# Scaling a pass's tokens on one engine, and copying values in sixteen pieces: a change to the projections of an encoder block

## The chip, the cores and the metric

One core of a Trainium2 chip runs the whole kernel in one launch. The metric is the device time of an execution in microseconds (us); smaller is better.

## The reference

The block prepends 16 learned meta tokens to 2048 tokens of width 1024, normalises them, projects them once, feeds two mixers side by side (attention in a window of a grid, and a gated delta rule in both directions), projects back, and ends with a gated feed-forward layer and a last normalisation.

```python
h = jnp.concatenate([meta, x], axis=1)
u = rmsnorm(h, g_mix[l])
proj = u @ w_in[l]
na_q, na_k, na_v, dn_q, dn_k, dn_v, dn_z, dn_b, dn_a = jnp.split(proj, pts, axis=-1)
y_na = neighbourhood_attention(na_q, na_k, na_v, na_rel_bias[l], rows)
y_dn = gated_deltanet(dn_q, dn_k, dn_v, dn_z, dn_b, dn_a, ...)
h = h + jnp.concatenate([y_na, y_dn], axis=-1) @ w_out[l]
u = rmsnorm(h, g_ffn[l])
h = h + (silu(u @ w_gate[l]) * (u @ w_up[l])) @ w_down[l]
return rmsnorm(h, g_final)[:, N_META:]
```

Here `rmsnorm(x, g)` is x times the reciprocal root mean square of its row, times g. What matters below are the projection `u @ w_in` and the values `na_v` of the attention's 8 heads.

## The kernel before

The change lies in `phase_a`, the projections, which take the first 890 us or so. Work there is done in two passes, each for half of the tokens; the pass for tokens 1024 to 2047 comes first, and the second pass (from about 400 us) has tokens 0 to 1023 with the meta tokens. Tokens lie in tiles of 128; the tiles of a pass are grouped into three chunks.

**Tokens of a pass.** Both a high and a low part of each normalised token are kept in fp32r (`uh`, `ul`), and products are made three times: high by high, high by low, low by high. In the second pass the reciprocal norms are known already (`rb`, a row copied to all partitions, held in the buffer that the trace calls `gb`) and the input comes transposed, features on partitions. `put_t` (from L310) loads a tile `xt` of 128 x (8 feature blocks x 128 tokens), multiplies it by the feature gains `gc` on POOL (L321), multiplies it by `rb` on DVE (L322), casts the high part on ACT (L324), and subtracts for the low part on DVE (L325). The pool of these tiles has three buffers, so the first three tiles of the second pass are scaled long before it starts and five at its start, as the buffers come free.

**Units.** A pass is a list of units. A feature unit (`dense_feat`, products at L405) makes 128 output features for the three chunks, 72 products in all; a token unit (`run_nat`, products at L429) makes 256 or 272 output columns for each token tile, 24 products a tile. Both write an accumulator `acc` in PSUM, which has three buffers. ACT evacuates it (L447 and L472 for token units, L490 for feature units); DVE adds to some of them (L473). Behind a feature unit come a short convolution (ACT L497, DVE L499), a gate (ACT L632, DVE L633), transposes on TensorE (L639) and squares on ACT (L642). The weights of a unit are loaded ahead by `weights`: two transfers to `raw` tiles, of which there are two buffers (L236), a cast of the high part on ACT (L241, to `wf` or `wn`), and the low part on POOL (L242).

**Side work.** Between chunks, `step` (L376) advances generators that are held in `Side` queues: the weights `ws`, the work after a convolution `post`, the preparation of the delta rule `pre`, and `first`. `pre` builds triangular inverses: it loads `dx` (L840) and rows of gates (L843), stores blocks to memory and reads them back as lanes (L905 and L907 write `lane`, L916 reads the blocks `U`, `af`, `ab` from it), multiplies small blocks on TensorE (L938 and on, in three PSUM buffers `pp`) and stores `xq` (L994).

**Values.** The attention's values are projected by two token units, four heads each. `evac_v` stores each tile to `S.vn` in device memory (L456). When a unit is done, `fin_v` (L462) copies it within device memory to `S.vx`, four copies of overlapping column ranges, with 24 or 32 columns of 64 values, for four heads at a time: each is a transfer of 136 rows (4 heads x 34 grid rows) of 1536 or 2048 numbers. These are read in the attention stage, after `phase_a`.

All these transfers are issued by SyncE (SP), in its order. The order of each engine is set by a scheduler when the program is built: it simulates the program and takes ready instructions by priority, so an edit can move instructions elsewhere. Queued work then runs in that order on each engine.

Of the kernel before, what the change touches and what calls it, by code (L numbers as in the profile page):

```python
# [12 lines left out]
ALU = mybir.AluOpType  # L13
# [3 lines left out]
P = 128  # L17
# [4 lines left out]
KB = 8  # L22
# [13 lines left out]
CLO, CN = (0, 8, 24, 40), (24, 32, 32, 24)  # L36
# [10 lines left out]
def bc(ap, shape):  # L47
    return ap.to_broadcast(shape)
# [144 lines left out]
def phase_a(tc, S, x, meta, x_t, xe_t, g_mix_b, g_mix_c, w_feat, w_nat0, w_nat, conv_w, a_log, dt_bias, handover):  # L193
# [3 lines left out]
    nc = tc.nc  # L197
    with ExitStack() as es:
# [17 lines left out]
        rb, gb = gb, gb[:, 0:D]  # L216
        gc_ = sm.tile([P, KB], F32, name="gc", bufs=1)
        U = Ctx()
        post, pre, first, ws = Side(True), Side(), Side(), Side()
        behind = Behind(tc)  # L220

        def weights(u):
# [61 lines left out]
        def prep_rs():  # L284

            for jobs in half_plan(0):
                for job in jobs:
                    if job[1] == P:
                        square(job, load_x(job), 0)
                        yield  # L290
            finish_rs(0, 8, P)
            yield

        def row_rs():

            pt = ptp.tile([P, 4, P], F32, name="tp")
            nc.tensor.transpose(pt[0:17, 0], rsx[:, 0:17], S.ident)
            row = sm.tile([17, P], F32, name="rsrow", bufs=1)
            nc.vector.tensor_copy(row, pt[0:17, 0])
            h = nc.sync.dma_start(S.rs, row)  # L300
            U.xe = sm.tile([P, KB, NM + 2], F32, name="xe", bufs=1)
            yield
            flat = S.rs.rearrange("a b -> (a b)").rearrange("(o n) -> o n", o=1)
            nc.sync.dma_start(rb[:, 0:HT + 2], bc(flat[:, 0:HT + 2], [P, HT + 2]))
            nc.sync.dma_start(rb[:, HT + 2:], bc(flat[:, 16 * P:16 * P + NM], [P, NM]))
            with tc.issue_after(h.ins):
                nc.sync.dma_start(U.xe, xe_t)
                nc.sync.dma_start(gc_, g_mix_c)
            yield

        def put_t(job, ci):

            r0, np_, off, is_meta = job
            if np_ < P:
                e = U.xe[:, :, 0:NM] if is_meta else U.xe[:, :, NM:NM + 2]
                o = HT + 2 if is_meta else r0
            else:
                e = xp.tile([P, D], F32, name="xt").rearrange("p (k t) -> p k t", k=KB)
                nc.sync.dma_start(e, x_t[r0 // P])
                o = r0  # L320
            nc.gpsimd.tensor_tensor(e, e, bc(gc_.rearrange("p (k o) -> p k o", o=1), [P, KB, np_]), ALU.mult)  # L321
            nc.vector.tensor_tensor(e, e, bc(rb[:, o:o + np_].rearrange("p (o t) -> p o t", o=1), [P, KB, np_]), ALU.mult)  # L322
            uh, ul = (v[ci][:, :, off:off + np_] for v in (U.h, U.l))
            nc.scalar.copy(uh, e)  # L324
            nc.vector.tensor_tensor(ul, e, uh, ALU.subtract)  # L325

# [18 lines left out]
        def build(half, known):  # L345
            U.plan = half_plan(half)
            U.h, U.l = [], []
            for ci, jobs in enumerate(U.plan):
                U.h.append(upool.tile([P, KB, UCOL[ci]], F32R, name=f"uh{ci}"))
                U.l.append(upool.tile([P, KB, UCOL[ci]], F32R, name=f"ul{ci}"))  # L350
                if known:
                    with tc.high_priority(600):
                        for job in jobs:
                            put_t(job, ci)
                    continue
                xs = []
                for n, job in enumerate(sorted(jobs, key=lambda j: -j[1])):
                    xs.append((job, load_x(job)))
                    if ci == 0 and n == 0:
                        nc.sync.dma_start(gb, bc(g_mix_b, [P, D]))  # L360
                        load(0)
                if ci == 0:
                    nc.sync.dma_start(cw, conv_w)
                    nc.vector.tensor_scalar(cw, cw, 0.5, None, op0=ALU.mult)
                for n, (job, xt) in enumerate(xs):
                    square(job, xt, half, ci == 0 and n == 1)
                cs = [rcol(job, half) for job, xt in xs]
                if ci > 0:
                    finish_rs(min(cs), max(cs) + 1, P)
                for n, (job, xt) in enumerate(xs):  # L370
                    if ci == 0:
                        finish_rs(cs[n], cs[n] + 1, P)
                    put(job, xt, ci, half, n != 3)

        def step():
            ws.step()  # L376
            post.step()
            pre.step()
            first.step()

        def tick():
            behind.run(step)

        def drain(*sides):
            while any(s.q for s in sides):
                tick()
# [4 lines left out]
        def load(u):  # L391
            while u not in W:
                ws.step(True)
# [45 lines left out]
        def run(u, ci):  # L439
            (run_feat if units[u][0] == "f" else run_nat)(u, ci)  # L440
# [19 lines left out]
            return f  # L460

        def fin_v(h0):  # L462
            def f():
                for C in range(4):
                    nc.sync.dma_start(S.vx[C][h0:h0 + 4].rearrange("h r c d -> h r (c d)"),
                                      S.vn[h0:h0 + 4, :, CLO[C]:CLO[C] + CN[C]].rearrange("h r c d -> h r (c d)"))
            return f

        def evac_z(zi):
# [106 lines left out]
        for pi, us in enumerate(passes):  # L576
            if pi == 0:
                build(1, False)
                post.add(prep_rs())
            else:  # L580
                build(0, True)
            n = len(us)

            m = 3 if pi == 0 else 2
            groups = [list(range(m))] + [[i] for i in range(m, n)]
            for gi, grp in enumerate(groups):
                if pi == 1 and gi == len(groups) - 1:
                    drain(post, first)
                    early.close()
                    handover()  # L590
                if pi == 0 and gi == 13:
                    first.add(row_rs())
                for i in grp:
                    load(u0 + i)
                for ci in range(3):
                    for i in grp:
                        run(u0 + i, ci)
                if us.index(v0s[pi]) in grp and pi == 0:
                    pre.add(gates(tc, S, Q, 1, a_log, dt_bias))
                    pre.add(pre_unit(tc, S, Q, 0, 1), lambda: post.done >= 5)  # L600
                    pre.add(pre_unit(tc, S, Q, 1, 1), lambda: post.done >= 9)
                if us.index(v0s[pi]) in grp and pi == 1:
                    pre.add(gates(tc, S, Q, 0, a_log, dt_bias))
                    pre.add(pre_unit(tc, S, Q, 0, 0), lambda: post.done >= 17)
                    pre.add(pre_unit(tc, S, Q, 1, 0), lambda: post.done >= 21)
                    first.add(meta_state(tc, S, Q, cv, ptp), lambda: post.done >= 25)
            u0 += n
# [1264 lines left out]
@with_exitstack  # L1872
def block_kernel(ctx: ExitStack, tc: tile.TileContext, x, meta, x_t, xe_t, g_mix, g_mix_c, w_feat, w_nat0, w_nat, conv_w, rel, a_log,
                 dt_bias, norm_g, w_out, g_ffn, w_gate, w_up, w_down, g_final, out):
    S = scratch(tc, ctx)
    with ExitStack() as es:
        scratch_ab(tc, S, es)
        att = []
        phase_a(tc, S, x, meta, x_t, xe_t, g_mix, g_mix_c, w_feat, w_nat0, w_nat, conv_w, a_log, dt_bias,
                lambda: att.append(attention_loads(tc, S, es, rel)))  # L1880
        wes = ctx.enter_context(ExitStack())
        W = wes.enter_context(tc.tile_pool(name="W", bufs=2 * KEEP, side="right", reuse_waits="tile"))
        c = phase_c(tc, S, W, wes, x, w_out, g_ffn, w_gate, w_up, w_down, g_final, out)
        phase_b(tc, S, att[0], W, norm_g, lambda: next(c))
    for _ in c:
        pass
# [19 lines left out]
```

## Time and profile before

| | |
|---|---|
| median of 3 executions | 2893.03 us (2889.85 to 2894.18) |
| the profiled execution | 2883.66 us |
| its span in the trace | 2881.9 us |
| granted clock of TensorE, mean | 0.97 |
| TensorE (PE) busy | 2740.7 us, 95% |
| VectorE (DVE), ScalarE (ACT), GpSimd (POOL) busy | 61%, 41%, 26% |
| moved by DMA | 462.15 MB |

Times in the trace are counted from the start of the span. The granted clock is a share of full speed: 1.00 is 2.4 GHz, 0.50 is 1.2 GHz. A wait is idle time of an engine in front of one instruction, with what released it; "SPq" is the stream of instructions with which SyncE issues transfers. The DMA share of a stretch is the mean busy share of the core's 16 DMA engines in it.

### The profile page before, as it was taken

How to read it: one execution, taken by the hardware profiler on the slowest of the kernel's cores; microseconds unless marked ns; L12 is line 12 of the kernel's file. 1: busy time of each engine (PE TensorE's matmuls, PEld its weight loads, DVE VectorE, ACT ScalarE, POOL GpSimd, SP SyncE). 2: the span in 40 equal slices, each digit the busy share in tenths (PEclk: the TensorE clock that was granted, in tenths of full speed). 3: DMA queues.
4: the chain of work that ended last, by engine and by line, in shares of the span. 5: the costliest groups of instructions: out<-in, count | busy, mean ns of one | idle time of the engine just before them, and what ended most of it. 6: DMA issues, size and time to landing. Idle time of an engine off the chain costs nothing.

```text
span 2881.9 us, 45992 instructions
## 1 busy us (share of the span) xinstructions
PE 2740.7 (95%) x16364; PEld 2400.2 (83%) x16364; DVE 1758.0 (61%) x3916; ACT 1170.4 (41%) x2741; POOL 744.4 (26%) x809
## 2 busy tenths in 40 slices
PE   8999988988988999979999999999999999999998
PEld 8999988988888988878887888877887888888886
DVE  5897467895643556764567566554548556654354
ACT  4652333652415667752334333243434333233342
POOL 2253353341511212221134322300104322220010
PEclk9999999999989999989999999999999999999999
DMA  4675654565769888985534222246353222225452
GB/s 151 189 205 142 163 165 135 172 179 172 211 159 287 265 229 254 291 281 156 176 126 163 81 88 80 81 131 246 128 176 119 80 86 88 74 95 201 143 179 70
DMA packets 385220, 462.15 MB, mean 160 GB/s; under 512 B 93492, under 2 KB 277133, under 8 KB 383423
## 3 DMA queue, kind: packets, MB, share of 16 engines
q1 hardware_dynamic: 383262, 452.92, 51.5%
q0 software_dynamic: 1728, 6.29, 0.6%
q8 instruction: 130, 2.13, 0.3%
q14 instruction: 100, 0.81, 0.1%
HBM read 329.95 MB, written 136.95 MB: 162 GB/s over the span
## 4 chain that ended last, share of the span: by engine, by line
PE 54%; DMA 3%; DVE 2%; ACT 0%; issue 0%; POOL 0%; SPq 0%; DVEq 0%; ACTq 0%; POOLq 0%
PE pg L1609 24%; PE pg L1685 8%; PE pd L1469 6%; PE pd L1685 4%; PE tp L1685 4%; PE pd L1609 4%; DMA rt<-ut 1%; DMA z<-zx 1%; PE y L1148 1%; DMA k<-kx 0%; PE tp L1495 0%; PE tp L1416 0%; DMA qr<-qx 0%; DVE w L1453 0%; PE y L1134 0%
## 5 line engine op out<-in xcount | busy, mean ns | idle before, releaser
L405 PE MATMUL acc<-uh,wf 128*128 128x384 f32 (+5 forms) x1920 | 469.2, 328 | 2.3 <-ACT uh L342 1.1
L1609 PE MATMUL pg<-T,w 128*128 128x512 f32 x1584 | 393.2, 397 | 2.6 <-ACT T L1452 1.4
L1453 DVE TENSOR_TENSOR w<-rw,w 128x512 fp32r<-128x512 f32 x308 | 241.1, 785 | 251.4 <-ACT w L1452 250.5
L1609 PE MATMUL pg<-B,w 128*128 128x512 f32 x1584 | 388.6, 398 | 3.6 <-ACT B L1452 3.0
L1452 ACT CAST w<-rw 128x512 fp32r<-128x512 f32 x308 | 190.2, 620 | 485.5 <-PE tp L1685 253.4
L1609 PEld LDWEIGHTS pg<-B,w 128*128 128x128 f32 x1584 | 299.1, 189 | 77.9 <-ACT B L1452 3.9
L1609 PEld LDWEIGHTS pg<-T,w 128*128 128x128 f32 x1584 | 298.0, 188 | 76.4 <-ACT T L1452 1.8
L405 PEld LDWEIGHTS acc<-uh,wf 128*128 128x128 f32 x1920 | 339.5, 192 | 4.9 <-ACT uh L342 1.2
L405 PE MATMUL acc<-ul,wf 128*128 128x384 f32 (+5 forms) x960 | 312.3, 325 | 0.0
L1557 POOL TENSOR_TENSOR s<-rw 128x512 f32<-128x512 f32 x88 | 120.4, 1369 | 548.0 <-DMA rw<-in_w_gate_dram 297.8
L1685 PE MATMUL pg<-w,hT 128*128 128x512 f32 x1056 | 260.8, 395 | 1.2 <-ACT hT L1452 1.1
L1685 PEld LDWEIGHTS pg<-w,hT 128*128 128x128 f32 x1056 | 198.1, 188 | 50.0 <-ACT hT L1452 1.5
L429 PE MATMUL acc<-wn,uh 128*128 128x256 f32 (+3 forms) x1056 | 210.7, 298 | 8.5 <-DVE vs L473 8.2
L1453 DVE TENSOR_TENSOR w<-s,w 128x512 fp32r<-128x512 f32 x176 | 131.6, 750 | 137.9 <-ACT w L1452 136.8
L1452 ACT CAST w<-s 128x512 fp32r<-128x512 f32 x176 | 108.5, 620 | 233.5 <-PE pg L1609 138.4
L405 PEld LDWEIGHTS acc<-ul,wf 128*128 128x128 f32 x960 | 184.3, 192 | 1.0 <-DVE ul L343 0.2
L429 PEld LDWEIGHTS acc<-wn,uh 128*128 128x128 f32 (+1 forms) x1056 | 173.3, 197 | 11.4 <-DVE vs L473 8.7
L429 PE MATMUL acc<-wn,ul 128*128 128x256 f32 (+3 forms) x528 | 158.0, 299 | 2.3 <-DVE rx_i L58 2.3
L1469 PE MATMUL pd<-w,yh 128*128 128x512 f32 x512 | 160.0, 394 | 0.0
L499 DVE SCALAR_TENSOR_TENSOR ct<-cr,cw,ct 128x1024 f32<-128x1024 f32 (+1 forms) x96 | 136.4, 1426 | 37.7 <-ACT ct L497 36.5
L242 POOL TENSOR_TENSOR wf<-raw,wf 128x512 fp32r<-128x512 f32 x80 | 117.7, 1486 | 154.9 <-ACT wf L241 131.6
L1623 DVE TENSOR_TENSOR eg<-pg,eg 128x512 f32<-128x512 f32 x110 | 75.9, 690 | 106.4 <-PE pg L1609 106.3
(359 smaller groups left out, 5305.0 us busy)
## 6 DMA issues: line engine op xcount, KB each, us to landing
rw<-in_w_down_dram SPq DMA_DIRECT2D x88, 512.0 KB
w<-dx SPq DMA_DIRECT2D x24, 1024.0 KB
rw<-in_w_gate_dram SPq DMA_DIRECT2D x44, 512.0 KB
rw<-in_w_up_dram SPq DMA_DIRECT2D x44, 512.0 KB
hd<-eg SPq DMA_DIRECT2D x88, 256.0 KB
s<-hd SPq DMA_DIRECT2D x88, 256.0 KB
raw<-in_w_feat_dram SPq DMA_DIRECT2D x80, 256.0 KB
xq<-xq SPq DMA_DIRECT2D x32, 512.0 KB
```

The source lines that it names most:

```text
L242: nc.gpsimd.tensor_tensor(lo, raw, hi, ALU.subtract)
L405: nc.tensor.matmul(ps[:, 0:c1 - c0], hl[:, a, k, :], (U.h, U.l)[l][ci][:, k, c0:c1], start=(i == 0), stop=(i == 23))
L429: nc.tensor.matmul(ps[0:np_, 0:n], (U.h, U.l)[l][ci][:, k, off:off + np_], hl[:, a, k, 0:n], start=(i == 0), stop=(i == 23))
L499: nc.vector.scalar_tensor_tensor(tt, raw[:, j:j + T], cw[:, b, j:j + 1], tt, op0=ALU.mult, op1=ALU.add)
L1148: nc.tensor.matmul(po, t.pT[0:w, c], t.v[0:w, c], start=(c == 0), stop=(c == nch - 1))
L1452: nc.scalar.copy(dst_h, src)
L1453: eng.tensor_tensor(dst_l, src, dst_h, ALU.subtract)
L1469: nc.tensor.matmul(ps, (yh, yl)[a][:, k], wo[k][:, b, cs], start=(i == 0), stop=(i == 23))
L1557: nc.gpsimd.tensor_tensor(s, p, q, op)
L1609: nc.tensor.matmul(ps, w[:, a, k], t[:, b, k], start=(k == 0 and (a, b) == (0, 0)), stop=(k == 3 and a == 1))
L1623: nc.vector.tensor_tensor(dst, ps, x0, ALU.add)
L1685: nc.tensor.matmul(acc[j][hf], hk[f][:, a, j * P:(j + 1) * P], wk[f][hf][:, b], start=(f == 0 and i == 0), stop=(f == NFF - 1 and i == 2))
```

## The change

First, `put_t` scales a tile by eight instructions of VectorE, one a feature block of 128 x 128, each by the gain of its feature (a scalar for each partition) and by `rb`. GpSimd has no part in it any more. Second, `fin_v` no longer issues its four copies. It adds a generator to a new `Side`, `cps`, that issues a copy for each column range and head, 16 in all with 34 rows each, and asks for two steps between one and the next; `step` advances it, and the drain before the last unit includes it.

```diff
@@ phase_a
-        post, pre, first, ws = Side(True), Side(), Side(), Side()
+        post, pre, first, ws, cps = Side(True), Side(), Side(), Side(), Side()
@@ put_t
-            nc.gpsimd.tensor_tensor(e, e, bc(gc_.rearrange("p (k o) -> p k o", o=1), [P, KB, np_]), ALU.mult)
-            nc.vector.tensor_tensor(e, e, bc(rb[:, o:o + np_].rearrange("p (o t) -> p o t", o=1), [P, KB, np_]), ALU.mult)
             uh, ul = (v[ci][:, :, off:off + np_] for v in (U.h, U.l))
+            for k in range(KB):
+                nc.vector.scalar_tensor_tensor(e[:, k], e[:, k], gc_[:, k:k + 1], rb[:, o:o + np_], op0=ALU.mult, op1=ALU.mult)
             nc.scalar.copy(uh, e)
             nc.vector.tensor_tensor(ul, e, uh, ALU.subtract)
@@ step
             first.step()
+            cps.step()
@@ fin_v
         def fin_v(h0):
+            def copies():
+                for C in range(4):
+                    for h in range(h0, h0 + 4):
+                        yield 2
+                        nc.sync.dma_start(S.vx[C][h].rearrange("r c d -> r (c d)"),
+                                          S.vn[h, :, CLO[C]:CLO[C] + CN[C]].rearrange("r c d -> r (c d)"))
+
             def f():
-                for C in range(4):
-                    nc.sync.dma_start(S.vx[C][h0:h0 + 4].rearrange("h r c d -> h r (c d)"),
-                                      S.vn[h0:h0 + 4, :, CLO[C]:CLO[C] + CN[C]].rearrange("h r c d -> h r (c d)"))
+                cps.add(copies())
             return f
@@ the loop over units
-                    drain(post, first)
+                    drain(post, first, cps)
```

Lines below the first edit stand a few lines lower in the changed kernel (L465 is L468, L473 is L479, L840 is L846, L843 is L849, L905 is L911, L907 is L913, L916 is L922, L994 is L1000; L322 is L323; L236 stays). Three places in the order of the engines speak of the change.

SyncE after the first value unit of the second pass: the last stores of values, the copies, and what follows up to the weights that the unit at about 553 us uses. Before:

```order
L456 DMA vn<-vs 128x4x64 x2
L840 DMA ul<-dx 128x2x256 x2
L465 DMA vx_59<-vn 136x1536
L465 DMA vx_60<-vn 136x2048
L465 DMA vx_61<-vn 136x2048
L465 DMA vx_62<-vn 136x1536
L994 DMA xq<-U_3814 128x8x128
L840 DMA af<-dx 128x2x256
L994 DMA xq<-U_3815 128x8x128
L671 DMA mkT<-ct 128x16
L994 DMA xq<-U_3814 128x8x128
L664 DMA dx<-ct 128x8x128
```

And with the change:

```order
L457 DMA vn<-vs 128x4x64 x2
L846 DMA ul<-dx 128x2x256 x2
L468 DMA vx_59<-vn 34x1536 x4
L468 DMA vx_60<-vn 34x2048 x4
L468 DMA vx_61<-vn 34x2048 x4
L468 DMA vx_62<-vn 34x1536 x4
L1000 DMA xq<-U_3814 128x8x128
L846 DMA af<-dx 128x2x256
L1000 DMA xq<-U_3815 128x8x128
L677 DMA mkT<-ct 128x16
L1000 DMA xq<-U_3814 128x8x128
L670 DMA dx<-ct 128x8x128
```

The sixteen pieces stand in a row where the four copies stood. In both orders a load `ab<-dx` and a store `xq<-U` follow, and then the two loads of `raw<-in_w_feat_dram`.

SyncE after the second value unit, where the lanes of the inverses (`lane`) and the blocks read back from them (`U`, `af`, `ab`) stand next to the copies. Before, behind the copies of `vx_59` and `vx_60`:

```order
L465 DMA vx_61<-vn 136x2048
L465 DMA vx_62<-vn 136x1536
L905 DMA lane_79<-yl 128x1024
L907 DMA lane_79<-ul 128x1024
L916 DMA U_6419<-lane_79 32x16x32 x4
L916 DMA af<-lane_79 32x16x32 x2
L916 DMA U_6420<-lane_79 32x16x32 x4
L916 DMA af<-lane_79 32x16x32
L916 DMA ab<-lane_79 32x16x32 x3
L840 DMA ul<-dx 128x2x256
L843 DMA yl<-grow 128x256
L236 DMA raw<-in_w_nat_dram 128x512
```

And with the change, behind four pieces of `vx_59`, the first lane transfer (L911), four pieces of `vx_60` and one block of `U`:

```order
L913 DMA lane_79<-ul 128x1024
L922 DMA U_6479<-lane_79 32x16x32 x3
L922 DMA ab<-lane_79 32x16x32 x3
L849 DMA yl<-grow 128x256 x2
L922 DMA af<-lane_79 32x16x32 x2
L922 DMA U_6480<-lane_79 32x16x32 x4
L922 DMA af<-lane_79 32x16x32
L846 DMA ul<-dx 128x2x256 x2
L849 DMA yl<-grow 128x256 x2
L468 DMA vx_61<-vn 34x2048 x4
L468 DMA vx_62<-vn 34x1536 x4
L236 DMA raw<-in_w_nat_dram 128x512
```

Half of the pieces now stand ahead of the second lane transfer and half behind the blocks, directly in front of the weights of the next token unit.

VectorE at the start of the second pass, with the value bias (`vs`, L473 or L479) and the low parts (`ul_...`, L325). Before:

```order
L325 TENSOR_TENSOR ul_4915<-xt,uh_4914 128x8x128 x3
L473 SCALAR_TENSOR_TENSOR vs<-vs,acc 128x256 x2
L322 TENSOR_TENSOR xt<-xt,gb 128x1024
L325 TENSOR_TENSOR ul_4939<-xt,uh_4938 128x8x128
L322 TENSOR_TENSOR xt<-xt,gb 128x1024
L473 SCALAR_TENSOR_TENSOR vs<-vs,acc 128x256 x2
L322 TENSOR_TENSOR xt<-xt,gb 128x1024
```

And with the change:

```order
L325 TENSOR_TENSOR ul_4915<-xt,uh_4914 128x8x128 x3
L479 SCALAR_TENSOR_TENSOR vs<-vs,acc 128x256 x2
L323 SCALAR_TENSOR_TENSOR xt<-xt,gc,gb 128x128 x15
L325 TENSOR_TENSOR ul_4963<-xt,uh_4962 128x8x128
L323 SCALAR_TENSOR_TENSOR xt<-xt,gc,gb 128x128 x9
L479 SCALAR_TENSOR_TENSOR vs<-vs,acc 128x256 x2
L325 TENSOR_TENSOR ul_4963<-xt,uh_4962 128x8x128
```

The second pair of L473 stood behind the scaling of the fifth tile; it now stands behind that of the sixth too.

## Rows read from the trace of the kernel before

**Rows 1.** The page: busy time of each engine, share of the span.

```profile
PE 2740.7 (95%) x16364; PEld 2400.2 (83%) x16364; DVE 1758.0 (61%) x3916; ACT 1170.4 (41%) x2741; POOL 744.4 (26%) x809
```

**Rows 2.** Waits of TensorE, 395 to 760 us: total, times, longest.

```profile
PE tp L639 <- DVE ct L633: 11.9, 6, 4.9
PE acc L429 <- DVE vs L473: 8.2, 2, 4.8
PE pp L938 <- DMA af<-lane: 6.2, 1, 6.2
```

**Rows 3.** SyncE's issues around the second value copies: start, us, engine, line.

```profile
676.58 2.66 SPq L465 DMA_DIRECT2D vx<-vn  x4
679.29 0.63 SPq L905 DMA_DIRECT2D lane<-yl  x1
...
699.70 1.92 SPq L916 DMA_DIRECT2D U<-lane  x4
...
708.07 1.74 SPq L236 DMA_DIRECT2D raw<-in_w_nat_dram  x1
```

**Rows 4.** Waits of SyncE, 676 to 706 us: total, times, longest.

```profile
SPq L916 <- DMA lane<-yl: 18.5, 1, 18.5
```

**Rows 5.** Two stretches: us, busy of PE, PEld, DVE, ACT, POOL; PEclk, DMA share, GB/s.

```profile
680.40:683.20 2.80, 2.80 (x20) 2.80 (x19) 0.00 (x0) 0.45 (x1) 0.47 (x2) 1.00 0.96 399
684.00:698.50 14.50, 13.52 (x90) 13.20 (x88) 6.52 (x6) 5.28 (x10) 0.64 (x1) 1.00 0.51 210
```

**Rows 6.** DMA issues of 676 to 705 us, KB each.

```profile
vx<-vn SPq DMA_DIRECT2D x2, 1088.0 KB
vx<-vn SPq DMA_DIRECT2D x2, 816.0 KB
lane<-yl SPq DMA_DIRECT2D x1, 512.0 KB
```

**Rows 7.** SyncE's issues around the first value copies.

```profile
493.56 2.70 SPq L465 DMA_DIRECT2D vx<-vn  x4
512.79 0.37 SPq L994 DMA_DIRECT2D xq<-U  x1
...
530.28 1.59 SPq L236 DMA_DIRECT2D raw<-in_w_feat_dram  x2
```

**Rows 8.** ScalarE's timeline at the cast of those weights.

```profile
541.42 1.13 ACT L241 CAST wf<-raw 128x512 fp32r<-128x512 f32 x2
```

**Rows 9.** POOL's timeline there: their low parts.

```profile
542.10 2.54 POOL L242 TENSOR_TENSOR wf<-raw,wf 128x512 fp32r<-128x512 f32 x2 [10.60 <-PE tp L639]
```

**Rows 10.** TensorE's timeline at 552, 697 and 746 us.

```profile
552.71 0.46 PE L405 MATMUL acc<-uh,wf 128*128 128x258 f32 x2
...
697.25 0.27 PE L639 MATMUL tp<-ident,ct 128*128 128x128 f32 x1
703.74 0.31 PE L938 MATMUL pp<-af,U 32*32 32x32 f32 x2 [6.22 <-DMA af<-lane]
...
746.43 0.59 PE L429 MATMUL acc<-wn,uh 128*128 128x256 f32 x2
```

**Rows 11.** A stretch behind TensorE's wait at 697: columns as in rows 5.

```profile
701.00:711.30 10.30, 7.56 (x142) 7.08 (x143) 4.23 (x8) 1.15 (x2) 1.03 (x2) 0.50 0.75 139
```

**Rows 12.** ScalarE's timeline at the cast of the weights behind the second copies.

```profile
724.42 1.14 ACT L241 CAST wn<-raw 128x512 fp32r<-128x512 f32 x2
```

**Rows 13.** POOL's timeline at the start of the pass: the sixth tile.

```profile
414.94 2.14 POOL L321 TENSOR_TENSOR xt<-xt,gc 128x1024 f32<-128x1024 f32 x1 [0.70 <-DMA xt<-in_x_t_dram]
```

**Rows 14.** DVE's timeline, 385 to 440 us.

```profile
386.23 1.13 DVE L877 SCALAR_TENSOR_TENSOR U<-pp,beta,E 128x128 f32<-128x128 f32 x4 [5.90 <-POOL E L858]
...
387.93 1.26 DVE L853 TENSOR_SCALAR E<-ab,gc 128x128 f32<-128x128 f32 x6
...
411.26 1.23 DVE L322 TENSOR_TENSOR xt<-xt,gb 128x1024 f32<-128x1024 f32 x1 [5.57 <-POOL xt L321]
...
415.25 2.91 DVE L322 TENSOR_TENSOR xt<-xt,gb 128x1024 f32<-128x1024 f32 x1
```

## The prediction

> **What bounds the kernel now.** I read the page first. TensorE is busy 95% of the span [rows 1], so an edit on another engine can only win the waits in front of TensorE, and can lose by making new ones. So next the waits of TensorE for the second pass up to 760 us, where all of the change lies: 8.2 us for vector's L473 in two waits, 6.2 us at once for a block of inverses (`af`), 11.9 us for vector's L633 in six [rows 2]. The first 8.2 us is where the scaling sits: vector adds the value bias (L473) only after the tiles ahead of it in its order, and TensorE runs out of accumulators. The second is where the copies sit. Reader, follow it on SyncE: the four copies of the second value unit are issued at 676.58, the lane load L905 behind them at 679.29, and L916, which needs that load, only at 699.70 [rows 3], having waited 18.5 us for it [rows 4]. Then the use of the 16 DMA engines by stretch [rows 5]: 0.51 at 210 GB/s from 684 to 698.5, with the four copies in flight; 0.96 at 399 GB/s from 680.4 to 683.2, when the lane load runs beside them. I take three things from it. An engine moves about 26 GB/s in both states (399 over 0.96 x 16; 210 over 0.51 x 16). A copy of 136 rows keeps 8 engines of the 16 busy. And the four copies keep the same 8, though all are in flight: other sets would have brought the share up; the lane load (128 rows) runs on the idle engines in those first 2.8 us, and its share on the 8 lies behind the copies until their end.
>
> **The pieces.** The share of 0.51 is 136 rows, 8 x 17, on 8 engines, though an uneven deal could have used 9 to 16: the rows are dealt evenly. A piece has 34 rows, 2 x 17, so by an even deal it runs on **2 engines**, the same ones every time. No row shows a transfer of 34 rows, so I bound it by the nearest ones: were it dealt on all 16 as the 128-row load, a group would take 9 us; on 8 as the copies now, 18.5; on 2, four times that. I take 2, as the copies of 136 rows are the nearest row, of the same data; the other two are the first rival. The Trainium skill has a rule for this ("DMA: Bandwidth & Descriptors", section "Why a DMA increments its semaphore by 16 and not by 1"): a transfer uses the largest number of engines, up to 16, that divides the slowest dimension on both sides, and from a hardware queue the lowest-numbered ones. By it too the sum is that of 2 engines; it gives 8 for 136 rows, which agrees with the 0.51, and leaves the first rival no room.
>
> Price: a group is 2 x 1088 + 2 x 816 KB = 3.90 MB [rows 6]. Over the 18.5 us that the load behind it was waited for that is 211 GB/s, 26.3 per engine. On two engines it takes 3.90 / 52.7 = **74 us**: 4.0 us for a piece of the narrow columns, 5.3 for one of the wide. What lies behind on those two engines waits, which is every transfer issued later, since all are issued by SyncE and have a share on them. "One every two dense chunks" does not help: in the order of the changed program the first group's 16 pieces still stand in a row on SyncE, and the second group's stand as 4, a lane load, 4, then eight in a row.
>
> *First group.* Before: issued at 493.56, next issue of SyncE at 512.79 [rows 7], so the copies ran from about 495 to 513.5. Now they run to 495 + 74 = 569. Behind them come eight transfers (four `xq` and one `dx` of 512 KB, two loads, one small), 3.1 MB: the two sixteenths of it on these engines are 0.39 MB, 7.5 us; then the `raw` pair of weights, issued before at 530.28 [rows 7], with 2 us to land: about 580. ScalarE casts them (541.42 before [rows 8]; the cast to the end of L242 took 3.2 us, to 544.6 [rows 9]), so the weights are whole at 584. The unit that needs them began at 552.8 [rows 10]. ScalarE takes its work in order, so the conv, the squares and the evacuations behind the cast wait too, and TensorE has three accumulators, just the unit's three chunks; it stops at about 553. Cost **+31**. Bounds: +18 if nothing of the eight delays the weights (7.5 less) and TensorE fills some 5 us of the pause with its transposes; +37 if a backlog of some 6 us on ScalarE comes on top. After a pause TensorE runs at half clock for some microseconds: 0.50 over 701 to 711.3 after a wait of 6.2 us [rows 11], 7.6 us of busy work there, so 3.8 lost. That wait had its loss already; a new one here costs **+3** (0 to 4).
>
> *Second group.* Start 676.6. Four narrow pieces end at 694.5; the first lane load lands at about 697, four wide pieces end at 717, the second lane load lands at 720. The `af` blocks read it, so TensorE's L938 goes at about 722.7 instead of 703.74 [rows 10]: +19. TensorE gets there earlier than before, since in the changed program's order 24 products of L405 (3.8 us, a unit's 72 taking some 12) now stand behind that point instead of ahead: they come after the wait, so +19 becomes **+23**. Then the last eight pieces, issued at about 727, need 37 us to 764.5. Right behind them stands the `raw` load of the next value-type weights, issued at 708.07 before [rows 3] and cast at 724.42 [rows 12]; now it lands at 767 to 768.5, while the shifted program wants it at 747.4. ScalarE then blocks for about 20 us. TensorE can go on until its accumulators and the three PSUM tiles of the inverses are full (some 3 to 8 us), and the unit that reads these weights came only 22 us after the cast, at 746.43 [rows 10], with a second round of loads between: 9 to 20 lost, I take **+17**. Together +40 (16 to 50), the ends being one of the two holds hidden, and both in full with ScalarE's backlog behind them. Another half-clock stretch: **+2**.
>
> **The scaling.** POOL's L321 (2.14 us for the sixth tile, [rows 13]) and vector's L322 (1.23 alone, 2.91 beside POOL [rows 14]) become 8 vector instructions of 128x128. No such instruction on this data is in the trace: the nearest are L853, six in 1.26 us (0.21), and L877, four in 1.13 with a PSUM operand (0.28) [rows 14], so 1.7 to 2.25 us a tile; I take 1.8, near L853, whose operands lie in SBUF too. Vector's bill per tile is then between 1.0 more than L322's alone and 1.2 less than L322's beside POOL, and POOL's 2 us ahead of it goes. But the second L473 pair moves behind all of the sixth tile's scaling, whose data came at 414.94 [rows 13]: 414.94 + 1.8, then the pair, which before followed L322's end at 418.16. The second wait, 4.8 us [rows 2], shrinks by about 1; the first, behind three L325s, stays. Three more of the waits for L633 follow a vector that is some 2 us ahead: **-2** for all of it (-5 to +3, the plus if the sixth tile's transfer comes late, as nothing of the pair passes it).
>
> *Sum.* -2 + 31 + 3 + 40 + 2 = 74; waits after the holds that are met while TensorE is late anyway (of the 11.9 us of L633 waits [rows 2]) give back about 4: **+70 us**. The profiled execution took 2883.66 us, so 2954 by its clock; it was the fastest shown, 9.4 below the median of 2893.03. I predict for the median: **2963**. A measurement tells from no change what is over 0.2%, 5.8 us.
>
> **Rivals.**
> *The pieces use other engines (faster).* If the 34-row pieces fall on different engines one after the other, or on 8 as the 136-row ones, a group still takes some 18 us or less; the lane load then stands behind four pieces (a quarter of the bytes) and not 16, so the 6.2 us wait goes, and its 3.8 us of half clock. With the scaling: -2 - 6 - 4 = -12, at 2881. For it: nothing in the trace shows a 34-row transfer. Against it: four copies in flight at once held the share at half. It decides from a copy rate above about 150 GB/s. Chance 0.05, with 0.04 for a result within 0.2% (a rate in between, where a loss of a few us meets the gain).
> *The holds are long, but mostly hidden.* The pieces take 74 us, yet the weights come in time because the eight transfers between do not wait in line, and only half of the second group bites: -2 + 18 + 0 + 16 + 2 - 4 = +30, at 2923. For it: the weights are issued 22 us ahead of use. Against it: 74 us is over three times that. Chance 0.14.
> *The holds grow.* If the late weights make the next loads late too, each unit of 12 us pays again until SyncE has caught up: +10 to +30 more, 2973 to 2993. For it: each raw buffer is one of two and is refilled only after its cast. Against it: once the pieces have drained, a 256 KB load needs 1 to 2 us. Chance 0.12.
> *The forecast as worked out*, 2935 to 2985: 0.65.
>
> The range takes the forecast, most of the hidden case and most of the growing one: 2918 to 2992. Faster 0.05, same 0.04, slower 0.91.
>
> **What would show it.** Right: in the stretch 495 to 569 the DMA share is down at 0.1 to 0.2, about 50 GB/s, where it was half; a group lasts some 70 us; the L241 cast of the unit at 553 waits for `raw` some 40 us; TensorE has a gap of about 30 us there, and one of about 20 at L938 behind `af`, and a third before the next value-type unit; L321 is gone from POOL, and vector's L473 waits are 1 to 2 us shorter. The prediction is wrong if the share stays at 0.4 or more with the pieces in flight, or if TensorE runs through 553 to 585 without a gap; the pieces then cost nothing, and the time is that of the first rival. It would be wrong on the second group if L938 goes within 5 us of the lane load's old landing.

## The result, and the profile after

The changed kernel takes 2956.65 us (median of 4, 2950.32 to 2960.61) against 2891.44 us before: a ratio of 1.0232, with a 95% interval of 1.021 to 1.0253. The change costs 65 us. The profiled execution took 2954.89 us, with a span of 2953.2 us, 71.3 longer than that of before.

The page, engines' busy time (before: [rows 1]):

```profile
PE 2746.8 (93%) x16364; PEld 2405.7 (81%) x16364; DVE 1755.2 (59%) x3986; ACT 1172.7 (40%) x2741; POOL 723.2 (24%) x799
```

TensorE is busy 6 us longer and idle 65 us longer. The waits of TensorE from 395 to 830 us (total, times, longest; before: [rows 2]) say where:

```profile
PE acc L406 <- ACT cr L496: 42.4, 2, 34.9
PE pp L944 <- DMA af<-lane: 30.5, 1, 30.5
PE tp L645 <- DVE ct L639: 20.0, 8, 7.7
PE acc L430 <- DVE vs L479: 9.1, 2, 8.0
```

The first of these waits, for a free accumulator, did not exist before. The second was 6.2 us. In time, TensorE's timeline (start, duration, and the idle time ahead in brackets; before: [rows 10]):

```profile
416.24 0.79 PE L430 MATMUL acc<-wn,uh 128*128 128x256 f32 x2 [8.01 <-DVE vs L479]
...
581.36 0.69 PE L406 MATMUL acc<-uh,wf 128*128 128x384 f32 x1 [34.87 <-ACT cr L496]
...
756.31 0.31 PE L944 MATMUL pp<-af,U 32*32 32x32 f32 x2 [30.53 <-DMA af<-lane]
...
806.20 0.58 PE L406 MATMUL acc<-uh,wf 128*128 128x256 f32 x1 [7.52 <-ACT cr L496]
818.94 1.11 PE L645 MATMUL tp<-ident,ct 128*128 128x128 f32 x4 [7.71 <-DVE ct L639]
```

ScalarE names what the accumulators waited for: the casts of weights (before: [rows 8, 12], with no wait ahead of them).

```profile
575.49 1.31 ACT L241 CAST wf<-raw 128x512 fp32r<-128x512 f32 x2 [40.21 <-DMA raw<-in_w_feat_dram]
...
802.10 0.62 ACT L241 CAST wn<-raw 128x512 fp32r<-128x512 f32 x1 [18.36 <-DMA raw<-in_w_nat_dram]
```

SyncE's timeline shows both groups of pieces and what stands behind them (before: [rows 3, 7]):

```profile
489.18 54.20 SPq L468 DMA_DIRECT2D vx<-vn  x16
543.49 4.15 SPq L1000 DMA_DIRECT2D xq<-U  x1
...
570.08 2.00 SPq L236 DMA_DIRECT2D raw<-in_w_feat_dram  x2
...
708.16 2.37 SPq L468 DMA_DIRECT2D vx<-vn  x4
710.57 0.42 SPq L911 DMA_DIRECT2D lane<-yl  x1
711.03 11.45 SPq L468 DMA_DIRECT2D vx<-vn  x4
...
728.53 7.90 SPq L913 DMA_DIRECT2D lane<-ul  x1
...
751.90 0.96 SPq L922 DMA_DIRECT2D af<-lane  x2
...
760.17 19.25 SPq L468 DMA_DIRECT2D vx<-vn  x8
779.53 4.16 SPq L236 DMA_DIRECT2D raw<-in_w_nat_dram  x1
```

SyncE itself is held there. All issues of copies, first before, then after (shortest, median and longest in ns, first and last start in us):

```profile
L465 SPq DMA_DIRECT2D vx<-vn x8: 600/625/725, 493.6 to 678.6; - x8
L468 SPq DMA_DIRECT2D vx<-vn x32: 533/2252/5972, 489.2 to 773.9; - x32
```

An issue took 0.6 to 0.7 us before and takes up to 6.0 us now. The four copies of the first group were issued in 2.70 us, its sixteen pieces take 54.20. So the weights behind them are issued only at 570.08 us, 39.8 later than the 530.28 of before, and ScalarE casts them 5.4 us after that: most of their wait lies ahead of their issue, in SyncE's stream.

Last, the stretches in which hardly anything but pieces moved (PEclk, DMA share and GB/s are the last three columns; before: [rows 5]), and the one behind the first hold:

```profile
493.00:538.00 45.00, 43.26 (x353) 41.21 (x354) 31.21 (x76) 22.50 (x58) 7.51 (x7) 0.92 0.13 55
714.00:724.00 10.00, 10.00 (x66) 10.00 (x65) 5.20 (x4) 2.50 (x4) 0.00 (x0) 1.00 0.13 53
765.00:775.00 10.00, 10.00 (x253) 8.98 (x250) 6.91 (x12) 3.53 (x6) 2.61 (x3) 0.94 0.14 57
582.00:599.00 17.00, 13.79 (x82) 13.56 (x82) 16.55 (x41) 10.28 (x34) 3.48 (x5) 0.80 0.56 158
```

0.13 of 16 engines is 2 engines, at 53 to 55 GB/s: some 26 an engine, as in [rows 5].

To see where the time was lost I compared, unit by unit, the start of its first product in both traces. The table has the shift of the changed kernel against before, from single profiled executions.

| place (start before) | shift |
|---|---|
| first feature unit of the second pass (423.8) | -2.4 |
| fourth (508.9) | -6.5 |
| the unit behind the first hold (552.8) | +28.5 |
| the next one (565.8) | +33.9 |
| the unit at the second copies (674.0) | +31.4 |
| L938, first product of the inverses (703.7) | +52.6 |
| second tile of the next token unit (750.5) | +77.5 |
| last token tile of the projections (879.3) | +78.3 |
| end of the span | +71.3 |

### The profile page after: what moved, and what is told of

The parts are those of the page before. It is cut to its first block, busy times and chain, and to the rows that moved or that the text cites. A ratio compares the mean times of both kernels' runs of the same rounds, so it can differ in the third digit from the quotient of the medians.

```text
span 2953.2 us, 46062 instructions
## 1 busy us (share of the span) xinstructions
PE 2746.8 (93%) x16364; PEld 2405.7 (81%) x16364; DVE 1755.2 (59%) x3986; ACT 1172.7 (40%) x2741; POOL 723.2 (24%) x799
## 4 chain that ended last, share of the span: by engine, by line
PE 58%; DMA 7%; DVE 4%; issue 1%; SPq 1%; ACT 1%; POOL 1%; DVEq 0%; ACTq 0%; POOLq 0%
PE pg L1615 23%; PE pg L1691 8%; PE pd L1475 6%; PE pd L1691 4%; PE tp L1691 4%; PE pd L1615 4%; DMA qr<-qx 2%; PE y L1154 2%; PE y L1140 1%; DMA xq<-xq 1%; PE z L1215 1%; DMA rt<-ut 1%; DMA b<-in_rel_dram 1%; PE z L1205 1%; PE z L1238 1%
```

## The experiments

Every kernel below was timed against the kernel before on the same chip. "Projections" is the shift in us at the end of the last product of the token units, which ends the projections in every version but the pieces on GpSimd; "rest" is what the span adds to it (difference of the spans less that shift). Both are from one profiled execution each; the ratio is from the timed runs. Executions of one version spread by up to 0.8%, and the profiled execution of the kernel before (2883.66 us) was 7.8 us faster than its median, so a few us in these two columns are not to be leaned on.

| version | rows of a transfer, queue | ratio (95%) | projections | rest |
|---|---|---|---|---|
| the change | 34, SyncE | 1.0232 (1.021 to 1.0253) | +78.3 | -7.0 |
| pieces alone | 34, SyncE | 1.0240 (1.0214 to 1.0265) | +76.7 | -2.9 |
| scaling alone | 136, SyncE | 0.9937 (0.9914 to 0.996) | -2.9 | -10.6 |
| pieces of 32 | 32, SyncE | 0.9941 (0.9916 to 0.9965) | -17.0 | +5.4 |
| copies of 128 | 128, SyncE | 0.9954 (0.9938 to 0.997) | -11.9 | +7.6 |
| second group alone | 136, then 34, SyncE | 1.0087 (1.0073 to 1.01) | +40.5 | -7.7 |
| pieces of 68 | 68, SyncE | 1.0066 (1.0052 to 1.0081) | +27.3 | +1.6 |
| pieces of 64 | 64, SyncE | 0.9955 (0.9942 to 0.9969) | -7.0 | -4.9 |
| copies of 128, old scaling | 128, SyncE | 0.9950 (0.9932 to 0.9969) | +6.2 | -6.7 |
| pieces on GpSimd | 34, GpSimd | 0.9967 (0.995 to 0.9984) | -25.8 | +26.4 |
| copies of 128 on GpSimd | 128, GpSimd | 0.9950 (0.9933 to 0.9967) | -0.9 | -3.9 |
| old copies on GpSimd | 136, GpSimd | 0.9945 (0.9926 to 0.9964) | -7.4 | -4.1 |

**The two parts apart.** The pieces with the old scaling (L321 and L322 put back):

> The sixteen pieces of 34 rows with the old scaling (POOL and vector). Theory (each piece runs on two DMA engines, and all later transfers wait behind it there): the whole loss is here, 2891 + 71 and a little more, since the scaling's gain of some 4 is missing: 2960 to 2972; DMA share near 0.15 at some 60 GB/s while a group runs. Rival A (the loss comes with the scaling, whose 80 instructions on vector reorder the engines): under 2920.

Measured: 2956.86 us, 1.0240; projections +76.7. A stretch within the first group, and TensorE's first hold:

```profile
500.00:540.00 40.00, 40.00 (x298) 38.03 (x298) 29.20 (x72) 21.28 (x56) 7.51 (x7) 0.93 0.13 54
```

```profile
580.11 0.69 PE L406 MATMUL acc<-uh,wf 128*128 128x384 f32 x1 [32.21 <-ACT cr L496]
```

The whole loss is in the pieces; the time lies 3 us under the band, which had counted on a gain of the scaling that the change then does not show. Rival A falls. And the scaling with the old copies:

```diff
-            nc.gpsimd.tensor_tensor(e, e, bc(gc_...), ALU.mult)
-            nc.vector.tensor_tensor(e, e, bc(rb[...]), ALU.mult)
+            for k in range(KB):
+                nc.vector.scalar_tensor_tensor(e[:, k], e[:, k], gc_[:, k:k + 1], rb[:, o:o + np_], op0=ALU.mult, op1=ALU.mult)
```

> The new scaling with the four old copies of 136 rows. Theory: in the changed kernel the units stood 2.3 us earlier behind the start of the pass and 6.5 us earlier at 502 us, before any piece was issued; part of it is met again by later waits, so 2884 to 2889. Rival A (the scaling is what costs): over 2920. Rival B (the lead is lost at the wait for the lanes behind the second copies): within 2 us of the kernel before.

Measured: 2871.62 us against 2888.82, 0.9937: 17 us faster, more than any theory had. Its waits of TensorE from 395 to 760 us:

```profile
PE acc L429 <- DVE vs L473: 8.4, 2, 6.1
...
PE pp L938 <- DMA af<-lane: 6.3, 1, 6.3
```

At the end of the projections it leads by 2.9 us only, near the 2 of the prediction; the lead of 7.5 us ahead of the second copies shrinks to 2.2 behind them, as rival B said, though the whole time is not within 2 us of before. By the profiled executions, the rest of its gain lies in the later stages, where the change has no line (see below). The parts do not add: TensorE waits 34.87 us at the first hold with the scaling's lead and 32.21 without it, so the lead is lost there.

**How many engines a transfer keeps.** The sixteen pieces, cut to 32 rows, with rows 32 and 33 in a transfer of their own:

```diff
-                        nc.sync.dma_start(S.vx[C][h]...
+                        nc.sync.dma_start(S.vx[C][h, 0:32]..., S.vn[h, 0:32, cs]...)
+                    nc.sync.dma_start(S.vx[C][h0:h0 + 4, 32:34]..., S.vn[h0:h0 + 4, 32:34, cs]...)
```

> As the changed kernel, but a piece has 32 rows instead of 34 (6% fewer bytes), and rows 32 and 33 of the four heads go in one small transfer for each column range: 20 transfers a group instead of 16. Theory (rows to engines): 32 rows are dealt on all 16 engines, a group takes some 10 us, DMA share 0.9 and near 400 GB/s while it runs, no cast waits 40 us for its weights: 2876 to 2890. Rival C (the number of transfers, or their place on SyncE, makes the holds): still 2940 to 2965.

Measured: 2872.11 us, 0.9941, 3.9 us under the band. A stretch within the first group, and the largest wait of TensorE for the lanes from 395 to 830 us:

```profile
485.00:493.00 8.00, 5.78 (x185) 5.60 (x175) 2.74 (x4) 1.36 (x3) 0.00 (x0) 0.71 0.87 273
```

```profile
PE pp L947 <- DMA af<-lane: 1.8, 2, 1.4
```

The share is near the expected 0.9, but at 273 GB/s and not near 400. Two rows fewer in a piece take 85 us off the change, though the sixteen pieces stand at the same places of SyncE's order. (The four small transfers of a group are issued far ahead of them, at 75 and 225 us.) Rival C falls. Then eight pieces a group, of 68 and of 64 rows, both at the same places of SyncE's order:

```diff
-                    for h in range(h0, h0 + 4):
+                    for h in (h0, h0 + 2):
                         yield 2
-                        nc.sync.dma_start(S.vx[C][h]...
+                        nc.sync.dma_start(S.vx[C][h:h + 2].rearrange("h r c d -> (h r) (c d)"), ...
```

> As the changed kernel, but a piece has the 68 rows of two heads: 8 transfers a group. 68 is 4 x 17. Theory (an even deal): 4 engines, DMA share near 0.27 and 105 GB/s, 37 us a group. The first group then drains by about 528 and its weights land before or near the moment they are cast, so that hold goes; in the second the lanes come some 18 us later than before (four of the pieces ahead of one lane, all of them ahead of the other), and the wait at the inverses is 20 to 28 us: 2890 to 2912, between the change and the version of 64 rows. Rival F (any cut of a copy costs alike): near 2956. Rival G (a piece's rows do not decide): as the version of 64 rows.

```diff
-                    for h in range(h0, h0 + 4):
+                    dst = S.vx[C][h0:h0 + 4].rearrange("h r c d -> (h r) (c d)")
+                    src = S.vn[h0:h0 + 4, :, CLO[C]:CLO[C] + CN[C]].rearrange("h r c d -> (h r) (c d)")
+                    for r0, r1 in ((0, 64), (64, 128), (128, 136)):
                         yield 2
-                        nc.sync.dma_start(S.vx[C][h]...
+                        nc.sync.dma_start(dst[r0:r1], src[r0:r1])
```

> The same 8 pieces in the same order of SyncE, of 64 rows each instead of 68, and the last 8 rows of the four heads in one small transfer for each column range. Theory: 64 rows run on 16 engines, 10 us a group, no hold and a shorter wait at the inverses than before. The stage of projections some 12 to 17 us shorter than before, and the order of TensorE in the attention stage is the one of the scaling alone, whose attention stage was 10 us shorter: 2860 to 2872. Rival: if that order does not matter, 2872 to 2880.

Measured: 2908.13 us (1.0066) with 68 rows, 2875.52 (0.9955) with 64. With 68 the first hold is gone, as expected: the unit behind it is 1.8 us earlier than before. A stretch within the second group, and the wait at the inverses; first 68 rows, then 64:

```profile
686.00:697.00 11.00, 11.00 (x73) 10.96 (x72) 6.65 (x7) 3.50 (x8) 0.15 (x1) 1.00 0.26 101
```

```profile
726.46 0.31 PE L944 MATMUL pp<-af,U 32*32 32x32 f32 x2 [26.81 <-DMA af<-lane]
```

```profile
667.00:677.00 10.00, 10.00 (x66) 10.00 (x66) 1.37 (x3) 2.52 (x4) 2.12 (x2) 1.00 0.91 322
```

```profile
691.45 0.31 PE L945 MATMUL pp<-af,U 32*32 32x32 f32 x2 [3.04 <-DMA af<-lane]
```

The shares make a series: 34 rows 0.13, 68 rows 0.26, 136 rows 0.51 [rows 5]; and 32 rows 0.87, 64 rows 0.91 with the lanes beside them. That is 2, 4 and 8 engines, and nearly 16. Rivals F and G fall. The version of 64 rows missed its band (2860 to 2872) by 3.5 us and lies in that of its rival, by which the order in the attention stage does not matter. The four old copies, cut into 128 and 8 rows:

> The new scaling, and the four copies of a group issued at once as before, but each cut into 128 rows and 8 rows. Theory: 128 rows run on 16 engines, so a group takes 9 to 10 us and not 18.5, and the lanes behind the second group come some 9 us earlier: the wait of 6.2 us of TensorE at the inverses goes: 2876 to 2886, the fastest of the four. Rival D (the copies then take bandwidth from the other transfers in flight, so the lanes come no earlier): as the scaling alone.

Measured: 2875.79 us, 0.9954, 0.2 under the band. TensorE's waits for the lanes are 0.4 us at most, where the scaling alone has 6.3, so the lanes come earlier and rival D falls. The time alone would not tell, since its interval overlaps that of the scaling alone. The projections are 11.9 us shorter. But it is not the fastest of the four: its later stages take 7.6 us more than before.

**The two groups apart.** The changed kernel, where `fin_v(0)` issues its four old copies:

```diff
             def f():
-                cps.add(copies())
+                if h0:
+                    cps.add(copies())
+                    return
+                for C in range(4):
+                    nc.sync.dma_start(S.vx[C][h0:h0 + 4]..., ...)
```

> As the changed kernel, but the first value unit is copied by the four old transfers of 136 rows; only the second goes in sixteen pieces. Theory: the first hold (35 us of the shift, between 553 and 581 us) goes and the second (some 48 us) stays, less 9 at the stage's end: 2915 to 2930. Rival E (the holds depend on each other: the second is so long only because the first has made everything late): under 2905.

Measured: 2914.44 us, 1.0087, and projections +40.5; the group's wait stays:

```profile
PE pp L949 <- DMA af<-lane: 30.2, 1, 30.2
```

The second group alone costs as much as it does behind the first (+47 from 31.4 to 78.3 there; here +47.8 from -7.3 to 40.5). Rival E falls: the holds add. The time is 0.6 us under the band.

**What the later stages add.** Where the changed code has no line, the last column differs from version to version, by 18 us without the pieces on GpSimd (for which see below). The copies of 128 rows with the old scaling were to tell whether the scaling does that:

> The kernel before with only its copies cut into 128 and 8 rows; the scaling is the old one. In the attention stage its order is nearly that of the scaling alone. Theory: the copies' part of the stage is won (6 to 10 us) and the attention stage is some 8 to 10 us shorter though the scaling is not touched: 2870 to 2880. Rival H (the later 10 us of the scaling alone come from the scaling itself): 2881 to 2886.

Measured: 2875.67 us, 0.9950, within the theory's band and not rival H's; the profiled execution took 2883.09 us, 7.4 more than the median, and shows the projections 6.2 us longer, against the expectation, and the rest 6.7 shorter. I compared the order of TensorE's instructions in the attention stage, row by row over 2000 of them. Eight versions (the change, pieces alone, scaling alone, second group alone, pieces of 64, copies of 128 with the old scaling, and the last two on GpSimd) agree with each other but for at most 50 rows, and the rest is shorter in all eight, by 2.9 to 10.6 us. Pieces of 32 and copies of 128 agree like that with the kernel before, and have +5.4 and +7.6; the remaining two (pieces of 68, pieces on GpSimd) have orders of their own. So an edit in the projections changes the order of a later stage, and these us go along with the order that the scheduler chose, whichever edit was made. That the order causes them is not shown: each is from a single execution, the kernel before has 0 in the order in which others have +5.4 and +7.6, and the 64 rows did not bear out the expectation that rested on it. What tips the order was not tried.

**Another queue.** The changed kernel's sixteen pieces, issued by GpSimd:

```diff
-                        nc.sync.dma_start(S.vx[C][h]...
+                        nc.gpsimd.dma_start(S.vx[C][h]...
```

> The changed kernel with the same sixteen pieces of 34 rows, issued by GpSimd in a queue of its own instead of SyncE. Theory: what holds the weights and the lanes is that they stand behind the pieces in one stream of issues, in line on the same engines; in a queue of their own the pieces hold nobody for their whole length: no cast waits 40 us for its weights, 2865 to 2895, with a loss only where GpSimd itself waits. Rival I (two engines that are full slow every transfer that has a share on them, whatever its queue): the holds stay, over 2930.

Measured: 2878.44 us, 0.9967, within the band. No hold is left. But the run does not tell what it was made for, because the pieces did not stay on two engines:

```profile
490.00:500.00 10.00, 7.18 (x89) 6.78 (x79) 2.69 (x5) 1.18 (x2) 6.83 (x15) 0.66 0.95 307
```

With the same 34 rows, 0.95 of the engines are busy at 307 GB/s, and the sixteen are issued within 13 us. From this queue the pieces spread; rival I was not tried. Its -25.8 and +26.4 in the table are not what the other rows have. In this version 224 products of the inverses, part of the projections, stand behind the last token unit, and the last of them ends at 882.8 us, where the projections before ended at 882.4. So the stage was not shortened by 26 us, and the attention stage did not give 26 us back, as the next expectation takes it. Two more versions asked whether both gains can be had:

> The new scaling, and the copies cut into 128 and 8 rows, issued by GpSimd in its own queue. TensorE's order in the attention stage is nearly that of the scaling alone, not that of the sixteen pieces on GpSimd, whose projections were some 26 us shorter and whose attention stage gave all of it back. Theory (stage by stage the two add up): projections 15 to 25 us shorter than before, attention 6 to 10 shorter: 2855 to 2872. Rival J (what the projections win, the attention stage always gives back, since something else sets the time at which it ends): 2875 to 2885.

> The new scaling, and the four old copies of 136 rows issued by GpSimd. Theory: if GpSimd's queue starts each transfer at other engines, as the 268 to 284 GB/s of its sixteen pieces of 34 rows say, two copies together use all 16 and a group takes some 10 to 13 us at a DMA share near 0.9; nothing on SyncE stands behind them; the attention order is that of the scaling alone: 2855 to 2872. If its copies stay on 8 engines, share near 0.5 and 18 us, with lanes that share them: 2868 to 2876.

Measured: 2870.33 us (0.9950) and 2869.97 us (0.9945), both within their bands, and both with the shorter rest; rival J (2875 to 2885) is not met. The second time lies in the bands of both its theories; the share tells them apart. In the second, copies of 136 rows from GpSimd fill the engines (from 490 to 500 us):

```profile
490.00:500.00 10.00, 6.37 (x128) 6.05 (x123) 2.74 (x4) 1.18 (x2) 1.50 (x3) 0.66 0.99 324
```

The profiled projections won 0.9 and 7.4 us, less than the 15 to 25 of the first expectation: that one met its band, but not by its sum. Seven versions lie 0.4 to 0.7% under the kernel before (the scaling alone, pieces of 32 and of 64, both of 128 on SyncE, and these two), and their intervals do not part them; the scaling alone is the smallest edit.

## Why the prediction was right

The forecast was 2963 us in a range of 2918 to 2992, and 2956.65 was measured. The sum was +70; 71.3 was measured between the profiled executions, 65 between the medians. Point by point, in its own terms and by the profiled executions:

- *A piece on two engines.* Right: 0.13 of the engines, 53 to 55 GB/s. The rule of the Trainium skill ("DMA: Bandwidth & Descriptors", "Why a DMA increments its semaphore by 16 and not by 1") agrees for SyncE's copies of 34, 68 and 136 rows (2, 4 and 8 engines by the rule, 0.13, 0.26 and 0.51 of 16 measured) and, with other transfers in flight, of 32 and 64 (16 by the rule, 0.87 and 0.91 measured).
- *First hold, +31 and +3.* Measured 35.0 (from -6.5 to +28.5) and 5.4 more in the next unit. The weights were cast at 575.5, not 580: the pieces began 4.4 us earlier (489.18), so the end came earlier by as much. TensorE, 6.5 us ahead by then, waited longer for nearly the same end. ScalarE waited 40.21 us where "some 40" stood. The 3 was too small: half clock and a wait of 3.2 us for the conv add up. No row of the prediction shows the 2 us from issue to landing that the sum takes for the weights, nor the 1 to 2 us that a rival takes; measured from issue to cast were 5.4 us (570.08 to 575.49). And most of the line that the weights wait in stands ahead of their issue, in SyncE, which the sum did not tell apart from a line on the two engines.
- *Second group, +23.* L944 went 52.6 us late, 21.2 more than the unit ahead of it; with the 24 products that came behind it (3.8 by the prediction) this is 25.
- *The weights behind the last eight pieces, +17 and +2.* Some 21: from 56.4 (52.6 and 3.8) to 77.5. ScalarE waited 18.36 us for the cast, "about 20" by the forecast, and TensorE then shows two waits of 7.5 and 7.7 us; from 806 to 819 us its granted clock is 0.63, where that stretch of the kernel before (737 to 750) has 1.00.
- *The scaling, -2.* Right at first (-2.4), by other terms. The step that was mis-sized is the price of an instruction: eight of 128x128 take 2.19 us, 0.27 each, near L877's 0.28 and not L853's 0.21. Vector's timeline has the fourth, the fifth and the sixth tile:

```profile
405.99 2.19 DVE L323 SCALAR_TENSOR_TENSOR xt<-xt,gc,gb 128x128 f32<-128x128 f32 x8 [3.44 <-DMA xt<-in_x_t_dram]
410.43 1.93 DVE L323 SCALAR_TENSOR_TENSOR xt<-xt,gc,gb 128x128 f32<-128x128 f32 x7 [2.26 <-DMA xt<-in_x_t_dram]
...
413.41 2.45 DVE L323 SCALAR_TENSOR_TENSOR xt<-xt,gc,gb 128x128 f32<-128x128 f32 x9
415.77 0.75 DVE L479 SCALAR_TENSOR_TENSOR vs<-vs,acc 128x256 f32<-128x256 f32 x2
```

  The data that came late were the fifth tile's (2.26 us waited at 410.43), not the sixth's, which the bounds had named: its eight stand in the nine at 413.41, with no wait. The pair of L479 came behind them at 415.77. Of TensorE's two waits for L479 the first shrank (3.5 to 1.1 us), which the forecast took to stay, and the second grew (4.8 to 8.0), which it took to shrink by 1: 9.1 us together, not the 7 or so expected (8.2 before). So the -2 was met by luck. Most of the lead came from later waits of the pass, where TensorE had gained 6.5 us by the fourth feature unit.
- *Recoveries, -4.* Between the holds 2.5 came back; the 7.0 us after the projections came from the attention stage and not from waits in this one.

The rivals: faster pieces did not occur on SyncE, and the holds were not hidden. Nor did unit after unit pay again, as the growing case has it: behind the first hold the shift stays at 33.9 us and then falls. The holds came out 10 us above the forecast all the same (+76 forecast, +86 measured), and the gains as well (-6 forecast, -15 measured, of which 7.0 in stages that the forecast did not look at). That the total is nearer to its forecast than the terms are is luck; the mechanism was right, and each hold's size was near.

## What to carry to other kernels

Cut a transfer by the number of engines that its rows divide on, not by its bytes: issued by SyncE, 34 rows ran on 2 of 16 engines, 32 rows on nearly all (a share of 0.13 and of 0.87). A small transfer that is slow holds everything behind it in the same stream, so look at what stands behind it, weights and lanes above all, before asking whether its own result is needed soon. And an edit in one stage of a scheduled program can change the order of a later one, and products can move past the mark by which a stage is timed: compare stage by stage, with repeated runs, and check that a mark has the same work ahead of it in every version.

## What was not expected

GpSimd's queue spread the same pieces of 34 rows over the engines (0.95 of 16, 307 GB/s, against 0.13 and 55 from SyncE) and gave copies of 136 rows 0.99. The scaling alone, forecast at 2 us, is 17 us faster (0.9914 to 0.996), most of it, by the profiled executions, outside the stage that it edits. Giving the copies all 16 engines brought the projections up to 17 us in a profiled execution, but no measurable gain beyond that of the scaling alone in the total.
